# Two gate projections with stationary tokens, and every engine in written order

## The chip, the core and the metric

The kernel runs on one core of a Trainium2 chip. A core has a matrix engine (PE), a vector engine (DVE), an activation engine (ACT), a general engine (POOL) and a queue engine that issues the DMAs (SP). The metric is the device time of one execution in microseconds, as the median of several.

## The reference

One layer of a hybrid decoder, 256 tokens of width 1024, all in float32:

```python
xn = rmsnorm(h, norm_mix_g[l])
q_a, k_a, v_a, q_b, f_b, i_b, og_b, g_a, g_b = split_cols(xn @ w_in[l])
y_a = moba_attention(q_a, k_a, v_a, positions) @ w_br_attn[l]
y_b = hgrn2(q_b, f_b, i_b, og_b, lb_all[l], hgrn_norm_g[l]) @ w_br_hgrn[l]
merged = jax.nn.sigmoid(g_a) * y_a + jax.nn.sigmoid(g_b) * y_b
h = h + merged @ w_out[l]
h = h + memory_cross_attention(rmsnorm(h, norm_x_g[l]), ...)
h = h + (jax.nn.silu(gu[..., :FFN_HIDDEN]) * gu[..., FFN_HIDDEN:]) @ w_ffn_out[l]
return rmsnorm(h, final_norm_g)
```

Two of the nine projections matter here. The forget gate of the gated recurrence is `lb + (1 - lb) * sigmoid(f_b)`, and its query is `silu(q_b) * 128 ** -0.5`; each has 8 heads of 128 features. The output of the recurrence is normed per head, so a constant factor on the query only changes the epsilon of that norm. The attention branch has 16 heads of 64 with rotary embedding; with 256 tokens there is one causal block.

## The kernel before

All weights pass through the core once, cut into 97 slabs of 128 x 2048 floats (1 MB each) in the order of `plan()`. `prep` loads a slab into `raw` (two buffers) and splits it into two float32r parts: `hi` by ACT (line 177) and `lo = raw - hi` (line 180), of which DVE takes 1152 columns and POOL 896 (`POOL_COLS`). `hi` and `lo` have three buffers each. `nxt()` hands out the next slab and first runs `prep` up to `LEAD` = 2 slabs ahead, so the split of slab i+2 is written just before the matmuls of slab i. Each product is three matmuls, hi·hi, hi·lo and lo·hi.

There are two forms of a product. `gemm_f` ("F") keeps weights stationary and streams 256 tokens; its result has features on partitions. `gemm_t` ("T") keeps tokens stationary and streams 512 weight columns; its result has tokens on partitions, and two slabs (`kh` 0 and 1) make one result of 512 columns. The forget gate and the recurrence queries, the first eight slabs, are in F form, because the recurrence wants features on partitions (`fT`, `KS`, `QQ`, `QP`). The token scale of the first norm, `r_x`, is computed from the feature-major x by squares, additions and a matmul with ones, turned into a row (`rows_x`), and multiplied into each gate result.

Side work is written as generators. `tick()` runs after every slab: first what lies in `later`, then one step of each generator in `bg`. Such generators are `rope_tables` (sine and cosine), `hgrn` (18 steps of the recurrence's score matrix: `level_one`, `pair_levels`, `widen`, `level`), `attention` (calls `duo`, the softmax of two heads, at two of three ticks; a duo's probabilities are transposed one tick later, tile `aT`, and multiplied with the values two ticks later, tile `ao`), `hgrn_out` (per head group: recurrence output `ho`, copy, square, norm, then transposes `hT`), and `memory`.

PE's instructions are issued in the order written. For the other engines a scheduler in the compiler chooses the order:

```python
with tc.manual_schedule(engines={mybir.EngineType.PE}):
    build(tc, aps, out)
```

In `duo` the two heads stand one after the other, and in `hgrn_out` the power comes ahead of the product that it does not need:

```python
G.tensor_tensor(r, v, nhalf, op=ALU.pow)
...
G.tensor_tensor(sg, on, sg, op=ALU.mult)
V.tensor_tensor(sg, sg, r.unsqueeze(2).to_broadcast([128, 4, 128]), op=ALU.mult)
```

Of the kernel before, what the change touches and what calls it, by code (L numbers as in the profile page):

```python
# [10 lines left out]
F32 = mybir.dt.float32  # L11
# [16 lines left out]
POOL_COLS = 896  # L28
WARM = 18
# [82 lines left out]
def build(tc, A, out):  # L112
    nc = tc.nc
    V, SC, G, PE, SY = nc.vector, nc.scalar, nc.gpsimd, nc.tensor, nc.sync
    with ExitStack() as ctx:
# [42 lines left out]
        def prep(tags=None, pieces=2, raw=None):  # L158
            i = made[0]
            made[0] += 1  # L160
            if raw is None:
                raw = wr.tile([128, 2048], F32, name="raw", tag="raw")
            if tags is None:
                hi = wh.tile([128, 2048], F32R, name="hi", tag="hi")
                lo = wl.tile([128, 2048], F32R, name="lo", tag="lo")
            else:
                hi = big(tags[0], "hix", (128, 2048), F32R)
                lo = big(tags[1], "lox", (128, 2048), F32R)
            n = 2048 // pieces
            if pieces == 2:  # L170
                SY.dma_start(raw, A["w"][i])
            for c in range(pieces):
                a = slice(c * n, (c + 1) * n)
                if pieces > 2:
                    SY.dma_start(raw[:, a], A["w"][i][:, a])
                    yield
                SC.activation(hi[:, a], raw[:, a], AF.Copy)  # L177
                cut = (c + 1) * n - POOL_COLS // pieces
                for eng, b in ((V, slice(c * n, cut)), (G, slice(cut, (c + 1) * n))):
                    eng.tensor_tensor(lo[:, b], raw[:, b], hi[:, b].bitcast(F32), op=ALU.subtract)  # L180
# [128 lines left out]
        opening = [prep(pieces=4), prep(pieces=4, raw=big("B14", "raw1", (128, 2048)))]  # L309
        for c in range(4):  # L310
            SY.dma_start(xraw[:, 2 * c:2 * c + 2], A["xT"][:, 2 * c:2 * c + 2])
            for g in opening:
                next(g)
            for k in (2 * c, 2 * c + 1):
                g1 = gv[:, V_MIX + k:V_MIX + k + 1]
                if k % 2 == 0:
                    SC.activation(Xh[:, k], xraw[:, k], AF.Copy, scale=g1)
                else:
                    V.tensor_scalar(Xh[:, k], xraw[:, k], g1, None, op0=ALU.mult)
                V.scalar_tensor_tensor(Xl[:, k], xraw[:, k], g1, Xh[:, k].bitcast(F32),  # L320
                                       op0=ALU.mult, op1=ALU.subtract)
# [21 lines left out]

        def ev_f(c):
            def ev(ps):
                for m in range(2):
                    h = 2 * c + m
                    t = t2("fraw", (128, 256))
                    V.tensor_tensor(t, ps[m] if isinstance(ps, list) else ps[:, m], rows_x, op=ALU.mult)
                    SC.activation(t, t, AF.Sigmoid)  # L350
                    V.tensor_scalar(fT[:, 2 * h:2 * h + 2].rearrange("p a b -> p (a b)"), t,
                                    oml[:, h:h + 1], lbt[:, h:h + 1], op0=ALU.mult, op1=ALU.add)
                SC.activation(KS[:, 4 * c:4 * c + 4], fT[:, 4 * c:4 * c + 4], AF.Copy, scale=-1.0, bias=1.0)
            return ev

        def ev_q(c):
            def ev(ps):
                t = t2("qraw", (128, 2, 256))
                th = t2b("qth", (128, 2, 256))
                V.tensor_tensor(t, ps, bc(rows_x, 2, 1), op=ALU.mult)  # L360
                SC.activation(th, t, AF.Tanh, scale=0.5)
                a = slice(4 * c, 4 * c + 4)
                v4 = "p m (a b) -> p (m a) b"
                V.scalar_tensor_tensor(QQ[:, a, 64:192], th.rearrange(v4, a=2), 1.0,
                                       t.rearrange(v4, a=2), op0=ALU.add, op1=ALU.mult)
                G.tensor_tensor(QP[:, a], QQ[:, a, 64:192], fT[:, a], op=ALU.mult)
                odd = QP[:, a].rearrange("p a (b c) -> p a b c", c=2)[:, :, :, 1]
                SC.activation(QQ[:, a, 0:64], odd, AF.Copy)
            return ev

        ws = [by_k(ready.pop(i), 8) for i in range(2)]
        at[0] = 2
        pss = [[p.tile([128, 256], F32, name="psg", tag=n) for _ in range(2)]
               for p, n in ((mm, "mm"), (sm, "sm"))]
        SY.dma_start(cst, A["cst"])
        run(prep())
        SY.dma_start(lm, A["lm"])
        SY.dma_start(posi, A["pos"])
        for k in range(8):
            for i in range(2):  # L380
                for m in range(2):
                    f_part(pss[i][m], ws[i], X, m, (k,))
        for c in range(4):
            square(xraw, c)
        feature_sum(xraw)
        w2 = by_k(nxt(1), 8)
        ps2 = mm.tile([128, 2, 256], F32, name="psf", tag="mm")
        f_part(ps2[:, 0], w2, X, 0, range(8))
        r_x = feature_rstd(xraw, "x")
        f_part(ps2[:, 1], w2, X, 1, range(8))  # L390
        w3 = by_k(nxt(1), 8)
        ps3 = mm.tile([128, 2, 256], F32, name="psf", tag="mm")
        f_part(ps3[:, 0], w3, X, 0, range(8))
        f_part(ps3[:, 1], w3, X, 1, range(7))
        rows_x = rows_of(r_x, "x", "rowsA")
        f_part(ps3[:, 1], w3, X, 1, range(7, 8))
        for c, ps in enumerate(pss + [ps2, ps3]):
            ev_f(c)(ps)
        r_half = cp.tile([128, 2], F32, name="r_half")
        V.tensor_scalar(r_half, r_x, 0.5, None, op0=ALU.mult)  # L400

# [4 lines left out]
        def rope_tables():  # L406
            posf = small("posf", [2])
            V.tensor_copy(posf, posi)
            q = cp.tile([128, 6, 2, 32], F32, name="rt")
            ang, m, mh, ml, r, t = (q[:, i] for i in range(6))  # L410
            for i in range(2):
                V.tensor_scalar(ang[:, i], cst[:, C_IF:C_IF + 32], posf[:, i:i + 1], None, op0=ALU.mult)

            def rnd(o, src, c):
                V.tensor_scalar(o, src, c, None, op0=ALU.mult)
                V.tensor_scalar(o, o, RND, None, op0=ALU.add)
                V.tensor_scalar(o, o, RND, None, op0=ALU.subtract)
# [6 lines left out]
            V.tensor_scalar(mh, mh, 1024.0, None, op0=ALU.mult)  # L424
            V.tensor_tensor(ml, m, mh, op=ALU.subtract)
# [11 lines left out]
            V.tensor_scalar(t, r, lim, -TWO_PI, op0=ALU.is_gt, op1=ALU.mult)  # L437
            V.tensor_scalar(ml, r, -lim, TWO_PI, op0=ALU.is_lt, op1=ALU.mult)
            V.tensor_tensor(r, r, t, op=ALU.add)
            V.tensor_tensor(r, r, ml, op=ALU.add)  # L440
            yield 1
            V.tensor_scalar(r, r, lim, -lim, op0=ALU.min, op1=ALU.max)
            V.tensor_scalar(t, r, -1.0, None, op0=ALU.mult)
            V.tensor_tensor(t, t, r, op=ALU.max)
            V.tensor_scalar(t, t, -1.0, TWO_PI / 4, op0=ALU.mult, op1=ALU.add)
            SC.activation(m, r, AF.Sin)
            SC.activation(mh, t, AF.Sin)
            for i in range(2):
                rs = r_x[:, i:i + 1]
                for c in range(2):  # L450
                    V.tensor_scalar(Ct[:, i, c * 32:(c + 1) * 32], mh[:, i], rs, None, op0=ALU.mult)
                V.tensor_scalar(St[:, i, 0:32], m[:, i], rs, -1.0, op0=ALU.mult, op1=ALU.mult)
                V.tensor_scalar(St[:, i, 32:64], m[:, i], rs, None, op0=ALU.mult)
# [129 lines left out]
        def hgrn_out(obh, obl):  # L583
            for g in range(2):
                for t in range(2):
# [15 lines left out]
                    V.tensor_scalar(v, ssq, 1.0 / 128.0, 512.0 * EPS, op0=ALU.mult, op1=ALU.add)  # L601
# [16 lines left out]

        hg = hgrn()
        for c in range(4):  # L620
# [122 lines left out]
        drain(hg)  # L743
# [35 lines left out]
        SY.dma_start(H, A["xtok"])  # L779
# [329 lines left out]
```

## Time and profile before

| | |
|---|---|
| median of 3 runs | 639.62 us (639.62 to 640.02) |
| the profiled execution | 641.26 us, span 639.5 us |
| busy share of the span | PE 98%, DVE 63%, ACT 50%, POOL 58% |
| first matmul of the first slab | 7.39 us |
| end of the eight slabs of gate and queries | 65.8 us |
| last matmul | 632.1 us |

The span runs from the first to the last instruction of the profiled execution; its own time is 1.8 us longer. PE's busy time contains pipelined matmuls that overlap, so the price of a matmul is read from the distance between two starts.

### The profile page before, as it was taken

The numbers are of one execution on the slowest core, as the hardware profiler recorded it, in microseconds if no ns is written. First come the engines' busy times: TensorE is split into PE (matmuls) and PEld (weight loads), VectorE is DVE, ScalarE is ACT, GpSimd is POOL, SyncE is SP. The second block draws the span as 40 slices with busy tenths as digits, with TensorE's granted clock in tenths as the row PEclk, the third lists the DMA queues.
The fourth block names the chain that finished last, engine by engine and source line by source line (L and its number), as shares of the span: only waits on it lengthen the run. The fifth ranks groups of instructions, "written<-read, shape, count | busy, mean of one in ns | idle before, by whom it ended". The sixth has DMA issues, their size and how long they took to land.

```text
span 639.5 us, 9044 instructions
## 1 busy us (share of the span) xinstructions
PE 624.7 (98%) x3428; PEld 533.6 (83%) x3428; DVE 405.9 (63%) x713; ACT 321.5 (50%) x506; POOL 369.4 (58%) x258
## 2 busy tenths in 40 slices
PE   8989999999999999999999999999999999999995
PEld 7979888888887877778889999888888888888884
DVE  6996898789857777695556546764344444444433
ACT  5383564433368666673446445564444444444433
POOL 3468654376554664346766767656565555665552
PEclk9998999999999999999999999999999999999998
DMA  8634554444443333545545455462355554555511
GB/s 282 216 128 162 197 198 169 157 166 138 152 179 132 132 132 132 181 149 197 180 155 192 148 197 183 165 248 81 133 197 198 181 175 178 194 194 197 198 67 66
DMA packets 17036, 107.56 MB, mean 168 GB/s; under 512 B 2144, under 2 KB 2272, under 8 KB 4576
## 3 DMA queue, kind: packets, MB, share of 16 engines
q1 hardware_dynamic: 16992, 106.98, 47.2%
q8 instruction: 27, 0.44, 0.3%
q14 instruction: 17, 0.14, 0.1%
HBM read 105.92 MB, written 1.05 MB: 167 GB/s over the span
## 4 chain that ended last, share of the span: by engine, by line
PE 91%; DVE 3%; POOL 2%; issue 2%; DMA 1%; ACT 1%; SPq 0%; POOLq 0%; DVEq 0%
PE pst L220 13%; PE pst L222 13%; PE pst L221 13%; PE psi L222 6%; PE psi L220 6%; PE psi L221 6%; PE psf L217 3%; PE psf L216 3%; PE psf L215 3%; PE acc L222 3%; PE acc L220 3%; PE acc L221 3%; PE lp L524 2%; PE pso L220 1%; PE pso L222 1%
## 5 line engine op out<-in xcount | busy, mean ns | idle before, releaser
L180 POOL TENSOR_TENSOR lo<-raw,hi 128x448 fp32r<-128x448 f32 (+1 forms) x194 | 298.5, 1554 | 207.9 <-ACT hi L177 198.2
L177 ACT ACTIVATE hi<-raw 128x1024 fp32r<-128x1024 f32 (+1 forms) x194 | 195.6, 1036 | 189.6 <-PE pst L222 79.3
L180 DVE TENSOR_TENSOR lo<-raw,hi 128x576 fp32r<-128x576 f32 (+1 forms) x194 | 197.4, 1021 | 122.5 <-ACT hi L177 121.3
L220 PE MATMUL pst<-hi,Xh 128*128 128x512 f32 x224 | 90.5, 404 | 0.0
L222 PE MATMUL pst<-hi,Xl 128*128 128x512 f32 x224 | 87.4, 390 | 0.0
L221 PE MATMUL pst<-lo,Xh 128*128 128x512 f32 x224 | 87.3, 390 | 0.0
L220 PE MATMUL psi<-hi,h2h 128*128 128x512 f32 x176 | 69.6, 395 | 0.0
L222 PE MATMUL psi<-hi,h2l 128*128 128x512 f32 x176 | 68.6, 390 | 0.0
L221 PE MATMUL psi<-lo,h2h 128*128 128x512 f32 x176 | 68.5, 389 | 0.0
L222 PEld LDWEIGHTS pst<-hi,Xl 128*128 128x128 f32 x224 | 42.0, 188 | 9.0
L220 PEld LDWEIGHTS pst<-hi,Xh 128*128 128x128 f32 x224 | 42.1, 188 | 8.7 <-issue 0.7
L221 PEld LDWEIGHTS pst<-lo,Xh 128*128 128x128 f32 x224 | 42.1, 188 | 7.9
L222 PEld LDWEIGHTS psi<-hi,h2l 128*128 128x128 f32 x176 | 33.0, 188 | 7.1
L221 PEld LDWEIGHTS psi<-lo,h2h 128*128 128x128 f32 x176 | 33.1, 188 | 6.6
L220 PEld LDWEIGHTS psi<-hi,h2h 128*128 128x128 f32 x176 | 33.1, 188 | 6.5
L220 PE MATMUL acc<-hi,hid 128*128 128x512 f32 x88 | 34.3, 390 | 0.0
L222 PE MATMUL acc<-hi,hid 128*128 128x512 f32 x88 | 34.2, 389 | 0.0
L221 PE MATMUL acc<-lo,hid 128*128 128x512 f32 x88 | 34.2, 389 | 0.0
L217 PE MATMUL psf<-Xh,lo 128*128 128x256 f32 x96 | 29.3, 306 | 4.1 <-DVE lo L180 2.2
L215 PE MATMUL psf<-Xh,hi 128*128 128x256 f32 x96 | 28.6, 298 | 0.0
L216 PE MATMUL psf<-Xl,hi 128*128 128x256 f32 x96 | 28.3, 295 | 0.0
L1000 DVE SCALAR_TENSOR_TENSOR fu<-psi,r_h,fg 128x256 f32<-128x256 f32 x22 | 10.6, 484 | 26.0 <-ACT fg L998 25.8
(316 smaller groups left out, 1266.8 us busy)
## 6 DMA issues: line engine op xcount, KB each, us to landing
raw<-w SPq DMA_DIRECT2D x95, 1024.0 KB, 4.8
raw<-w SPq DMA_DIRECT2D x8, 256.0 KB, 5.6
xraw<-xT SPq DMA_DIRECT2D x4, 256.0 KB, 5.5
H<-xtok SPq DMA_DIRECT2D x1, 1024.0 KB, 8.7
mraw<-mT SPq DMA_DIRECT2D x1, 1024.0 KB, 5.6
out<-H SPq DMA_DIRECT2D x4, 256.0 KB, 2.2
gfin<-gfin SPq DMA_DIRECT2D x1, 512.0 KB, 6.5
cst<-cst SPq DMA_DIRECT2D x1, 272.0 KB, 5.7
```

The costliest lines, as they stand in the source:

```text
L177: SC.activation(hi[:, a], raw[:, a], AF.Copy)
L180: eng.tensor_tensor(lo[:, b], raw[:, b], hi[:, b].bitcast(F32), op=ALU.subtract)
L215: PE.matmul(ps, lh, rh, start=first, stop=False)
L216: PE.matmul(ps, lh, rl, start=False, stop=False)
L217: PE.matmul(ps, ll, rh, start=False, stop=last)
L220: PE.matmul(ps, xh, h, start=first, stop=False)
L221: PE.matmul(ps, xh, l, start=False, stop=False)
L222: PE.matmul(ps, xl, h, start=False, stop=last)
L524: PE.matmul(ps[:, j], KS[:, a0 + j], QQ[:, a0 + j], start=True, stop=True)
L1000: V.scalar_tensor_tensor(u, ps[:, 256:512], r, g, op0=ALU.mult, op1=ALU.mult)
```

## The change

Slabs 0 to 7 (forget gate, recurrence queries) go to T form. `turned` turns the token-major result back with PE transposes (four groups of eight), one or two ticks later, and evicts it from there. The gate's sigmoid becomes a tanh with the token scale inside the activation, `0.5 * (1 - lb)` and the offset in the eviction; the query's silu is a `Silu` activation (so the factor 2 that the old form carried is gone, and the epsilon of the head norm goes from 512 to 128 times). The squares of x come from the token-major input H, by ACT with an accumulator, and H is loaded at the start and not at the gates. The rotary tables are computed on POOL, with a product and a sum in place of each fused operation, and are spread over six ticks. For slabs 2 to 7 DVE takes all of `lo` (`ALONE`). The loads of x come in pieces of 1, 1, 2, 2 and 2 feature blocks. The recurrence's score steps start one slab later, and the draining call before its output is gone. ACT, DVE, POOL and SP, too, issue in the order written.

```diff
+ALONE = range(2, 8)
-    for name, base in (("f", 4), ("q", 3)):
-        order += [("F", "w_in", base * 1024 + c * 256) for c in range(4)]
-    for base in (5, 2, 0, 1, 6):
+    for base in (4, 3, 5, 2, 0, 1, 6):
...
-                cut = (c + 1) * n - POOL_COLS // pieces
+                cut = (c + 1) * n - (0 if i in ALONE else POOL_COLS // pieces)
...
+        PIECES = (0, 1, 2, 4, 6, 8)
+        for a, b in zip(PIECES, PIECES[1:]):
+            SY.dma_start(xraw[:, a:b], A["xT"][:, a:b])
+            for k in range(a, b):
+                next(opening[k // 4])
+                part_x(k)
...
+        def turned(th, c, use):
+            def turn():
+                for b in range(2):
+                    bk = bank("fT_", (128, 2, 256))
+                    for j in range(2):
+                        for t in range(2):
+                            PE.transpose(bk[:, j, t * 128:(t + 1) * 128],
+                                         th[t][:, (2 * b + j) * 128:(2 * b + j + 1) * 128], ident)
+                    use(4 * c + 2 * b, bk)
+            later.append(lambda: later.append(turn))
...
+            def ev(t, ps):
+                th[t] = t2("fth")
+                SC.activation(th[t], ps, AF.Tanh, scale=r_half[:, t:t + 1])
+                if t == 1:
+                    turned(th, c, use)
...
+                SC.activation(th[t], ps, AF.Silu, scale=r_x[:, t:t + 1])
...
-        for c in range(4):
-            square(xraw, c)
-        feature_sum(xraw)
...
+        f2 = [mm.tile([128, 512], F32, name="pst", tag="mm") for _ in range(2)]
+        w = by_k(nxt(), 4)
+        for t in range(2):
+            t_part(f2[t], w, X, t, 0)
+        ssqx = small("ssqx", [2])
+        junk = big("B9", "junk", (128, 2, 1024))
+        for t in range(2):
+            SC.activation(junk[:, t], H[:, t], AF.Square, accum_out=ssqx[:, t:t + 1])
+        r_x = rstd_of(ssqx, "x")
...
             def acc(o, a, c, b):
-                V.scalar_tensor_tensor(o, a, float(c), b, op0=ALU.mult, op1=ALU.add)
+                G.tensor_scalar(u, a, float(c), None, op0=ALU.mult)
+                G.tensor_tensor(o, u, b, op=ALU.add)
...
+        start(rt)
+        for c in range(2):
+            gemm_t(X, ev_q(c))
         hg = hgrn()
-        for c in range(4):
-            if c == 2:
-                start(hg)
-            gemm_f(X, ev_q(c), bank("psf", (128, 2, 256)) if c == 0 else None)
-        start(rt)
+        next(hg)
+        start(hg)
...
-        drain(hg)
...
-        SY.dma_start(H, A["xtok"])
...
-        with tc.manual_schedule(engines={mybir.EngineType.PE}):
+        with tc.manual_schedule(engines={mybir.EngineType.PE, mybir.EngineType.Activation, mybir.EngineType.DVE,
+                                         mybir.EngineType.Pool, mybir.EngineType.SP}):
             build(tc, aps, out)
```

More of the change, by code (lines that the diff above doesn't have):

```diff
@@ L156, in build, with prep @@
         made, at = [0], [0]
-        def prep(tags=None, pieces=2, raw=None):
+        def prep(tags=None, raw=None):
             i = made[0]
             made[0] += 1
+            first = i < 2
             if raw is None:
@@ L168, in prep @@
                 lo = big(tags[1], "lox", (128, 2048), F32R)
+            pieces = 4 if first else 2
             n = 2048 // pieces
-            if pieces == 2:
+            if not first:
                 SY.dma_start(raw, A["w"][i])
@@ L173, in prep @@
                 a = slice(c * n, (c + 1) * n)
-                if pieces > 2:
+                if first:
                     SY.dma_start(raw[:, a], A["w"][i][:, a])
@@ L308, in build, with part_x @@
             PE.matmul(warm, still[:, :128], still, start=True, stop=True)
-        opening = [prep(pieces=4), prep(pieces=4, raw=big("B14", "raw1", (128, 2048)))]
-        for c in range(4):
[L311 to L321, printed above, removed]
+        opening = [prep(), prep(raw=big("B14", "raw1", (128, 2048)))]
+        def part_x(k):
+            g1 = gv[:, V_MIX + k:V_MIX + k + 1]
+            if k % 2 == 0:
+                SC.activation(Xh[:, k], xraw[:, k], AF.Copy, scale=g1)
+            else:
+                V.tensor_scalar(Xh[:, k], xraw[:, k], g1, None, op0=ALU.mult)
+            V.scalar_tensor_tensor(Xl[:, k], xraw[:, k], g1, Xh[:, k].bitcast(F32),
+                                   op0=ALU.mult, op1=ALU.subtract)
+        PIECES = (0, 1, 2, 4, 6, 8)
[4 more added lines that the diff above has]
+                part_x(k)
         for g in opening:
@@ L342, in build @@
         QP = big("B3", "QP", (128, 16, 128))
-        def ev_f(c):
[L345 to L353, printed above, removed]
+        gate_a = cp.tile([128, 8], F32, name="gate_a")
@@ L393, in build @@
[L393 to L398, printed above, removed]
+            h, l = (z[:, k % 4] for z in ws[k // 4])
+            for t in range(2):
+                PE.matmul(pss[t], Xh[:, k, t * 128:(t + 1) * 128], h, start=k == 0, stop=False)
+                PE.matmul(pss[t], Xl[:, k, t * 128:(t + 1) * 128], h, start=False, stop=False)
@@ new lines, in build @@
+            for t in range(2):
+                PE.matmul(pss[t], Xh[:, k, t * 128:(t + 1) * 128], l, start=False, stop=k == 7)
+        f2 = [mm.tile([128, 512], F32, name="pst", tag="mm") for _ in range(2)]
+        w = by_k(nxt(), 4)
+        for t in range(2):
+            t_part(f2[t], w, X, t, 0)
+        ssqx = small("ssqx", [2])
+        junk = big("B9", "junk", (128, 2, 1024))
+        for t in range(2):
+            SC.activation(junk[:, t], H[:, t], AF.Square, accum_out=ssqx[:, t:t + 1])
@@ L399, in build @@
+        r_x = rstd_of(ssqx, "x")
         r_half = cp.tile([128, 2], F32, name="r_half")
         V.tensor_scalar(r_half, r_x, 0.5, None, op0=ALU.mult)
+        for t in range(2):
+            ev_f0 = ev_f(0) if t == 0 else ev_f0
+            ev_f0(t, pss[t])
+        tick()
+        w = by_k(nxt(), 4)
+        ev_f1 = ev_f(1)
+        for t in range(2):
+            t_part(f2[t], w, X, t, 1)
+            ev_f1(t, f2[t])
+        tick()
         Ct = cp.tile([128, 2, 64], F32, name="Ct")
```

100 lines of the change are left out of this document (54 added, 46 removed).

## The prediction

> **What bounds the kernel now.** I read the page's busy times first, then who waited for whom on PE, then the stretches of time, and last the timelines of PE, DVE, ACT and POOL.
>
> ```profile
> PE 624.7 (98%) x3428; PEld 533.6 (83%) x3428; DVE 405.9 (63%) x713; ACT 321.5 (50%) x506; POOL 369.4 (58%) x258
> ```
> ```profile
> PE psf L217 <- DVE lo L180: 2.2, 3, 0.9
> PE psf L217 <- POOL lo L180: 1.8, 1, 1.8
> ```
> ```profile
> 21.78:65.82 44.04, 39.93 (x297) 38.40 (x296) 36.23 (x81) 22.38 (x34) 28.17 (x28) 0.92 0.45 164
> 44.31:47.72 3.41, 1.44 (x10) 1.03 (x8) 3.41 (x7) 2.84 (x4) 3.27 (x4) 0.97 0.00 0
> 47.50:50.90 3.40, 2.76 (x13) 2.76 (x14) 2.30 (x3) 0.00 (x0) 3.40 (x4) 0.50 0.56 149
> 50.90:54.30 3.40, 3.40 (x18) 3.40 (x18) 0.00 (x0) 0.00 (x0) 3.16 (x6) 0.50 0.38 159
> ```
> PE is the bound: 98% busy, and the two waits shown are all of its waits after the first block. They lie in the stage that the change rewrites: the forget gate's last two blocks and the four query blocks, 21.78 to 65.82 us. (A block is one 1 MB slab of weights.) Columns of a stretch are its length, then busy us of PE, weight load, DVE, ACT, POOL, then the granted clock. In 44.31 to 47.72 DVE is busy without a break while PE works 1.44 of 3.41 us; then the clock stands at 0.50 for 6.8 us. So what this stage pays is DVE arriving late, and then a slow clock. Behind it PE is full until its last matmul: there the change can only lose, unless it takes matmuls away, and it takes none away.
>
> **Part 1: matmuls.** The first eight blocks go from 48 matmuls of 256 columns to 24 of 512. Start times on PE give the price of each; the last row is eight transposes of 128 columns.
>
> ```profile
> 16.02 0.28 PE L215 MATMUL psg<-Xh,hi 128*128 128x256 f32 x1
> 16.14 0.28 PE L216 MATMUL psg<-Xl,hi 128*128 128x256 f32 x1
> ...
> 71.24 0.39 PE L220 MATMUL pst<-hi,Xh 128*128 128x512 f32 x1
> 71.47 0.39 PE L221 MATMUL pst<-lo,Xh 128*128 128x512 f32 x1
> ```
> ```profile
> 140.30 0.87 PE rT L656 x8
> ```
> 0.12 us x 48 = 5.76 us per block against 0.227 x 24 = 5.44: 0.3 us gained per block. The new tokens-by-features result has to be turned: four groups of eight transposes, 0.87 us each, say 1.0 with the change of operand type, so 4.0 us are added. By PE work alone, then, this is worth about nothing (eight blocks give 2.5); what counts is the stall and the clock.
>
> **Part 2: the front as a sum.** I leave the first two blocks where they end now, at 21.78 (the smaller pieces of x bring the first matmul a few tenths forward; the last quarter of slab 0 is now split after slab 1's third, which can take them back). Six blocks follow, 6 x 5.44 = 32.6, and four turns, 4.0: 36.6 us for what takes 44.04. Does everything else arrive? These rows carry it:
>
> ```profile
> raw<-w SPq DMA_DIRECT2D x95, 1024.0 KB, 4.8
> ```
> ```profile
> L177 ACT ACTIVATE hi<-raw 128x1024 fp32r<-128x1024 f32 x186 | 191.0, 1054 | 188.2 <-PE pst L222 79.3 <-PE psi L222 35.5 <-PE acc L222 28.0
> L753 ACT ACTIVATE tbt<-pst,r_half 128x512 f32<-128x512 f32 x4 | 2.7, 684 | 3.2 <-PE pst L222 3.0
> ```
> ```profile
> L271 POOL TENSOR_TENSOR r_x<-v__359,nhalf 128x2 f32<-128x2 f32 x1 | 0.7, 707 | 4.2 <-DVE v__359 L269 4.2
> ```
> Written order puts the squares of x, hence r_x, hence the forget gate's tanh, behind ACT's split of slab 4. That slab's buffer frees when slab 2 is split, about 20.5; 4.8 us to land gives 25.3; two halves of 1.05 give 27.4; two squares of 1024 columns, 1.05 plus about 0.2 for the accumulator each, 29.9; mean, power (0.7) and halving, 31.2; two tanh of 0.68, 32.6. PE wants to turn that gate at 21.8 + 2 x 5.44 = 32.7. The two meet; I allow 0.4 us of wait, so the front is 37.0 instead of 44.0: **-7.0 us**. If the slab lands 2 us later, -5; if the first blocks also gain a microsecond or two, -9.
>
> Removed from DVE: the rotary chain's small operations, the additions of the squares, the row scaling of eight gates and four queries. Added: all of `lo` for slabs 2 to 7. Alone, and beside POOL, a 576-column `lo` takes:
>
> ```profile
> 28.65 0.74 DVE L180 TENSOR_TENSOR lo<-raw,hi 128x576 fp32r<-128x576 f32 x1
> ...
> 35.87 1.44 DVE L180 TENSOR_TENSOR lo<-raw,hi 128x576 fp32r<-128x576 f32 x1 [0.19 <-ACT hi L177]
> ```
> ```profile
> L496 POOL TENSOR_TENSOR Tt<-Tt 128x64 f32<-128x64 f32 x2 | 0.6, 294 | 0.2
> ```
> Scaled to 1024 columns that is 1.3 to 2.6 us, 2.6 to 5.1 per slab, in a block of 5.44 plus a turn of 1.0 every other block or oftener, with slabs split two blocks ahead: it is hidden at the lower price, and nearly so at the upper. The rotary chain on POOL is about 55 operations near 0.3 us, 16 us spread over six blocks; nobody needs the tables before slab 16. [...] Early loading of H costs one 1 MB transfer, moved from one place to another.
>
> **Part 3: all engines as written.** This is where I expect the gain to go back. Today the scheduler weaves `lo` and other work into the waits of a softmax or a head norm. In written order each wait stands on DVE. The group that matters is `duo` (two heads' softmax, one after the other) followed in the same tick by a step of `hgrn_out`, then by the next `lo`. A duo, by its pieces:
>
> ```profile
> 212.81 0.28 DVE L679 CUSTOM_DVE_ANT_0 ap<-as,cst 128x128 f32<-128x128 f32 x1
> ...
> 213.01 0.42 DVE L679 CUSTOM_DVE_ANT_0 ap<-as,cst 128x256 f32<-128x256 f32 x1
> ...
> 216.47 0.16 DVE L682 TENSOR_SCALAR anm<-amx 128x2 f32<-128x2 f32 x1
> ...
> 217.68 0.17 DVE L686 RECIPROCAL asum<-asum 128x2 f32<-128x2 f32 x1 [0.40 <-ACT ap L684]
> 217.88 0.55 DVE L688 TENSOR_SCALAR ap<-ap,asum 128x128 f32<-128x128 f32 x2
> ```
> ```profile
> 222.54 0.40 ACT L684 ACTIVATE ap<-ap,anm 128x128 f32<-128x128 f32 x1 [0.34 <-DVE anm L682]
> ...
> 223.34 0.19 ACT L684 ACTIVATION_READ_ACCUMULATOR ap<-ap,anm 128x1 f32 x1
> ```
> Per head: reductions to 213.43 and the negation 0.15 make 0.77; exponentials from 222.54 to 223.53, 0.99, with DVE standing; reciprocal and scaling 0.75; 0.1 for the handshakes: 2.6 us, 5.2 for the two. A head-norm step:
>
> ```profile
> 225.28 0.58 ACT L596 ACTIVATE hon<-ho 128x512 f32<-128x512 f32 x1
> 225.88 0.63 ACT L598 ACTIVATE hsq<-hon 128x512 f32<-128x512 f32 x1
> ```
> ```profile
> 218.35 0.68 DVE L600 TENSOR_REDUCE hss<-hsq 128x4 f32<-128x512 f32 x1
> ...
> 220.38 0.69 DVE L606 TENSOR_TENSOR sog<-sog,hr 128x512 f32<-128x512 f32 x1 [1.15 <-POOL hr L602]
> ```
> ```profile
> 225.93 1.29 POOL L605 TENSOR_TENSOR sog<-hon,sog 128x512 f32<-128x512 f32 x1 [2.33 <-ACT hon L596]
> 228.25 1.01 POOL L602 TENSOR_TENSOR hr<-hv,nhalf 128x4 f32<-128x4 f32 x1 [1.02 <-DVE hv L601]
> ```
> Now L605 runs before L602 and DVE waits 1.15 us. In written order L605 stands behind the power, so DVE waits 2.5: 218.35 to 220.38, plus 1.3, plus 0.69 is 4.1, plus 0.5 for copy and square behind the last exponential, 4.6. With the slab's two `lo` (2 x 1.03 on the mean) a tick with both costs DVE 12 us. PE's ticks with such work last
>
> ```profile
> 210.56:218.67 8.11, 8.11 (x50) 6.46 (x50) 6.39 (x20) 5.87 (x14) 4.09 (x3) 1.00 0.52 156
> 218.67:227.74 9.07, 9.07 (x56) 7.32 (x54) 7.82 (x22) 6.51 (x16) 4.59 (x4) 1.00 0.40 145
> 227.74:235.72 7.98, 7.98 (x47) 6.41 (x46) 5.67 (x9) 4.86 (x8) 6.48 (x5) 1.00 0.32 111
> 235.72:244.73 9.01, 9.01 (x58) 7.36 (x58) 7.25 (x22) 5.83 (x14) 3.91 (x4) 1.00 0.36 119
> ```
> Ticks 1, 2 and 4 of these hold a duo and a norm step, 3 a norm step alone, 5 a duo. PE transposes a duo's probabilities one tick after its scores. Counting from 210.56: the first duo runs 2.2 to 7.4, norm to 12.1, `lo` to 14.2, the second duo to 19.4; PE wants it at 8.1 + 9.1 + 0.8 (another duo's output) = 18.0: **1.4 us**. Then norm 24.0, `lo` 26.1, norm 30.6, `lo` 32.7, third duo (0.4 of a split before it) 38.3; PE, now 1.4 late, wants it at 35.6: **2.7 us**. Norm 43.1, `lo` 45.2, fourth duo 50.4; PE wants it at 46.6: **3.8 us**. Together +7.9. With chains 15% shorter it is about 3, 15% longer 13. The next duos start on time again.
>
> Stalls of this size can drop the clock: the 6.8 us at half clock, shown above, behind a stretch with 1.44 of 3.41 us busy, lost 3.4. Half of that, 1.7, goes into the sum. [...]
>
> Elsewhere (gated recurrence, cross attention, feed-forward, end) each chain fits its tick in written order by my count; ends 0 and +3, value 0.
>
> **Sum.** -7.0 + 7.9 + 1.7 = +2.6 us. The profiled execution took 641.26 with a span of 639.5; the median is 639.62, and the difference carries over: 639.6 + 2.6 = **642.2 us**.
>
> **The rivals.** *A, the attention hides its waits:* the duo with norm and `lo` stays under PE's 8.5 us per tick instead of 12. For it speaks that before, with `lo` woven in, a duo was already done only a few tenths before its transposes; against it that weaving is what the change forbids. It decides at about 9 us. Then only the front counts: 632.6. *B, the front pays little:* POOL's small operations hold `lo` at its upper price, DVE needs 5.1 plus the evictions, a block runs up to 1 us late, four of them lose 4 us: front -3, total 646.2. *C, the stalls come without a half clock:* PE keeps working on either side of each, and the row that tripped was PE at 42% for a whole 3.4 us; -7.0 + 7.9 = +0.9, 640.5. [...] *D, written order is close to what the scheduler does anyway:* as A, and counted with it.
>
> **Chances.** Forecast 0.45 (its own range 638 to 647), A with D 0.27, B 0.15, C 0.13. About 0.2%, 1.3 us, is what a measurement of this kernel tells from no change. Faster: A, with 0.08 of the edges of forecast and C, 0.35. Same: 0.13, mostly C. Slower: 0.52. The range 632.0 to 648.5 reaches to A's middle and past B's.
>
> **What the changed profile would show.** Right: `pst` matmuls of X at 0.227 us from the start; the first `level_one` matmul (L478's line) not later than 65.8 - 7 plus its one-block shift; no half clock in the front; PE waiting on `aT` for the scaling of `ap` by DVE, three waits of 1 to 5 us some 200 us in; DVE waiting on POOL's `sog` 2.5 us. Wrong: no `aT` waits (A), or PE waits on `lo` or `fth` before 60 us (B). A wait of several microseconds elsewhere would break the zero that I gave to the rest.

## The result

| | median, us | lowest to highest | ratio to before (95% interval) |
|---|---|---|---|
| before | 639.62 | 639.25 to 640.02 | |
| after | 667.15 | 666.5 to 667.9 | 1.0431 [1.0413, 1.0449] |

The change makes the kernel 4.3% slower. Its profiled execution has a span of 665.1 us against 639.5, so 25.6 us have to be found in the two profiles (the medians differ by 27.5, mostly because the profiled execution before, 641.26 us, was 1.6 above its median). Two lines of the page and the list of what PE waited for, after:

```profile
span 665.1 us, 8697 instructions
PE 631.9 (95%) x3262; PEld 527.2 (79%) x3262; DVE 409.5 (62%) x653; ACT 325.0 (49%) x509; POOL 371.5 (56%) x294
```
```profile
PE psg L420 <- ACT hi L178: 4.7, 2, 3.6
PE aT L742 <- DVE ap L734: 3.6, 3, 1.9
PE ssq L298 <- issue: 3.0, 1, 3.0
PE psi L222 <- ACT hi L178: 2.5, 1, 2.5
PE hT L659 <- DVE amx L725: 2.4, 1, 2.4
PE psi L222 <- ACT h2h L1020: 1.9, 1, 1.9
...
PE ho L639 <- ACT pT L744: 1.3, 1, 1.3
PE psg L423 <- DVE lo L182: 1.1, 1, 1.1
PE hT L659 <- DVE obl L267: 1.1, 1, 1.1
```

Before, PE had two kinds of wait after its first block, 4.0 us together, both in the front. Now there are over a dozen, none longer than 3.6 us and spread from 10 to 480 us, nearly all on ACT or DVE (a transfer stands behind some of them, as will be seen). PE falls from 98% busy to 95%, and its busy time still grows by 7.2 us, though the program has 166 fewer matmuls (one of 512 columns does the work of two of 256): part of them ran at half clock. The windows view over six stretches of after (columns as in the prediction: length, busy us of PE, weight load, DVE, ACT, POOL, granted clock, DMA share, GB/s):

```profile
14.90:21.90 7.00, 5.79 (x13) 4.14 (x14) 6.47 (x17) 2.81 (x5) 2.04 (x3) 0.52 0.57 226
185.60:280.05 94.45, 84.80 (x459) 65.38 (x459) 61.20 (x164) 56.25 (x125) 39.73 (x28) 0.96 0.32 117
247.22:254.05 6.83, 6.23 (x22) 4.71 (x22) 4.38 (x5) 2.61 (x4) 4.90 (x4) 0.50 0.00 0
308.66:312.07 3.41, 3.41 (x10) 2.64 (x9) 2.80 (x6) 1.37 (x2) 0.81 (x2) 0.50 0.67 221
465.68:469.09 3.41, 3.41 (x9) 2.59 (x9) 3.41 (x3) 1.80 (x2) 3.41 (x3) 0.50 0.04 5
479.33:482.74 3.41, 3.41 (x9) 2.64 (x8) 1.44 (x3) 1.92 (x3) 3.05 (x3) 0.50 0.62 262
```

Where before had one stretch at 0.50, after has five, each behind a wait of PE, 24 us long in all; they cost half their length, 12 us, against 3.4 before.

That comparison leaves out one thing. The clock records of before begin only at 13.37 us; ahead of that the view prints 1.00, but the matmuls themselves start 0.21 us apart and not 0.12. From PE's timeline of before:

```profile
8.48 0.41 PE L216 MATMUL psg<-Xl,hi 128*128 128x256 f32 x1
8.70 0.41 PE L217 MATMUL psg<-Xh,lo 128*128 128x256 f32 x1
```

So before ran the first 26 matmuls of its opening at half speed too, which is about 26 x 0.09 = 2.4 us. After has its matmuls at full speed from the first one at 6.55 us, up to 15.1 us (those of 512 columns at 10.12, 10.34 and 10.57 us start 0.23 apart).

I divide the run where the same matmul first starts in each kernel: the third block's first matmul, the first attention score (`as`), the first matmul on `obh` (the recurrence's output), on `mh` (the two branches merged), into `pso` (the last projection added to H), into `psi` (feed-forward, in) and into `acc` (feed-forward, out). Stage lengths in us, from PE's start times:

| stage | before | after | difference |
|---|---|---|---|
| opening, two blocks | 21.78 | 25.91 | +4.1 |
| to the first attention score | 167.52 | 159.69 | -7.8 |
| attention and head norm | 80.34 | 94.45 | +14.1 |
| products on `obh` and `oah`, memory norm | 47.98 | 52.76 | +4.8 |
| memory and cross attention | 105.85 | 105.90 | 0 |
| `pso`, addition to H | 23.23 | 25.98 | +2.75 |
| first feed-forward block | 22.72 | 29.69 | +7.0 |
| the rest | 170.08 | 170.72 | +0.6 |

The rewritten front brings what it was meant to. It is lost again at five places, four of them in text that the change does not touch: only the order of issue differs there.

**The opening.** Timelines of ACT and of PE, after:

```profile
13.18 0.51 ACT L316 ACTIVATE Xh<-xraw,gv 128x256 fp32r<-128x256 f32 x1
13.83 1.77 ACT L178 ACTIVATE hi<-raw 128x512 fp32r<-128x512 f32 x3
```
```profile
15.03 0.74 PE L420 MATMUL psg<-hi,Xh 128*128 128x512 f32 x1 [3.60 <-ACT hi L178]
...
26.14 0.39 PE L223 MATMUL pst<-lo,Xh 128*128 128x512 f32 x1
26.37 0.39 PE L224 MATMUL pst<-hi,Xl 128*128 128x512 f32 x1
```

Slab 0's last quarter is the last of the three splits in the row at 13.83, because `run(opening[0])` stands behind all pieces of slab 1. PE stands 3.60 us for it and then runs at 0.52.

The late opening hides a second delay. DVE, ACT and PE, after:

```profile
20.13 2.35 DVE L182 TENSOR_TENSOR lo<-raw,hi 128x1024 fp32r<-128x1024 f32 x2
```
```profile
29.05 2.01 ACT L178 ACTIVATE hi<-raw 128x1024 fp32r<-128x1024 f32 x2 [4.07 <-DMA raw<-w]
34.41 1.27 ACT L385 ACTIVATE fth<-psg,r_half 128x512 f32<-128x512 f32 x2 [1.28 <-DVE r_half L434]
```
```profile
36.80 0.60 PE L363 MATMUL fT__359<-cst,fth 128*128 128x128 f32 x4
```

DVE's `lo` of slab 2 releases that slab's buffer at 22.5 us, and only then can slab 4's load start: it is issued at 22.51 and lands at 28.94. ACT stands for it until 29.05, and the gate's tanh, with the squares of x behind that split, ends at 35.7. PE comes to turn the gate at 36.80, so here it does not wait.

**The attention.** DVE and POOL in the first tick with a softmax pair and a norm step:

```profile
214.06 0.69 DVE L646 TENSOR_REDUCE hss<-hsq 128x4 f32<-128x512 f32 x1 [0.40 <-ACT hsq L644]
...
217.35 1.60 DVE L652 TENSOR_TENSOR sog<-sog,hr 128x512 f32<-128x512 f32 x1 [2.40 <-POOL sog L651]
```
```profile
216.05 1.26 POOL L651 TENSOR_TENSOR sog<-hon,sog 128x512 f32<-128x512 f32 x1
217.27 2.68 POOL L182 TENSOR_TENSOR lo<-raw,hi 128x448 fp32r<-128x448 f32 x2
```

DVE stands 2.40 us for POOL, and then its multiplication takes 1.60 us instead of 0.69: POOL's `lo` starts 0.08 us ahead of it and runs right across it. All four norm steps show this (1.60 to 1.64 us); before, one of four did (1.62 us, with POOL's `lo` starting 0.06 us ahead) and the other three took 0.69. In the same stretch PE's idle time is 94.45 - 84.80 = 9.65 us.

**Memory norm.** DVE's sum of squares stands behind a `lo`, and PE's `ssq` matmul, in written order too, blocks PE:

```profile
303.40 1.44 DVE L182 TENSOR_TENSOR lo<-raw,hi 128x576 fp32r<-128x576 f32 x1 [0.19 <-ACT hi L178]
304.76 1.62 DVE L292 TENSOR_TENSOR mraw<-mraw 128x512 f32<-128x512 f32 x1
306.41 1.23 DVE L293 TENSOR_TENSOR mraw<-mraw 128x256 f32<-128x256 f32 x1
```
```profile
307.75 0.58 PE L298 MATMUL ssq<-ones,mraw 128*128 128x1 f32 x4 [2.95 <-issue]
```

The view names no releaser ("issue"); the end of DVE's sum at 307.64 is the one that fits.

**First feed-forward block.** ACT, after:

```profile
462.96 0.63 ACT L876 ACTIVATE hjunk<-H 128x512 f32<-128x512 f32 x1 [2.21 <-DVE H L872]
...
463.59 3.88 ACT L178 ACTIVATE hi<-raw 128x1024 fp32r<-128x1024 f32 x4
472.86 2.01 ACT L178 ACTIVATE hi<-raw 128x1024 fp32r<-128x1024 f32 x2 [5.38 <-DMA raw<-w]
476.97 0.63 ACT L1020 ACTIVATE h2h<-h2g 128x512 fp32r<-128x512 f32 x1 [2.10 <-DVE h2g L1019]
```

No slab is split between the squares of H: the four halves follow in one go at 463.59, when PE already wants them (it waits 2.5 us there). The next slab's load could start only behind them (issued at 468.07 us, landed at 472.75), so ACT stands 5.38 us for it. `h2h` needs no load, but it needs `h2g` of DVE, and `h2g` stands in DVE's queue behind that slab's `lo`:

```profile
474.90 1.43 DVE L182 TENSOR_TENSOR lo<-raw,hi 128x576 fp32r<-128x576 f32 x1 [0.19 <-ACT hi L178]
476.26 0.68 DVE L1019 TENSOR_TENSOR h2g<-h2T,gv 128x512 f32<-128x512 f32 x1
```

PE waits 1.9 us for `h2h`.

### The profile page after: what moved, and what is told of

Same layout as the page of the kernel before. It is cut to its first block, busy times and chain, and to the rows that moved or that the text cites. A ratio compares the mean times of both kernels' runs of the same rounds, so it can differ in the third digit from the quotient of the medians.

```text
span 665.1 us, 8697 instructions
## 1 busy us (share of the span) xinstructions
PE 631.9 (95%) x3262; PEld 527.2 (79%) x3262; DVE 409.5 (62%) x653; ACT 325.0 (49%) x509; POOL 371.5 (56%) x294
## 4 chain that ended last, share of the span: by engine, by line
PE 83%; issue 4%; DVE 4%; POOL 3%; ACT 3%; DMA 2%; SPq 1%; POOLq 0%; ACTq 0%; DVEq 0%
PE pst L222 12%; PE pst L224 12%; PE pst L223 12%; PE psi L224 6%; PE psi L222 6%; PE psi L223 6%; PE acc L222 3%; PE acc L224 3%; PE acc L223 3%; PE psf L218 2%; PE psf L217 2%; PE psf L219 2%; DMA raw<-w 2%; POOL lo L182 2%; PE lp L570 2%
## 5 line engine op out<-in xcount | busy, mean ns | idle before, releaser
L182 POOL TENSOR_TENSOR lo<-raw,hi 128x448 fp32r<-128x448 f32 (+1 forms) x182 | 285.8, 1591 | 188.3 <-ACT hi L178 184.7
L182 DVE TENSOR_TENSOR lo<-raw,hi 128x576 fp32r<-128x576 f32 (+2 forms) x194 | 215.7, 1124 | 101.6 <-ACT hi L178 100.9
L222 PE MATMUL pst<-hi,Xh 128*128 128x512 f32 x272 | 110.0, 405 | 0.0
L223 PE MATMUL pst<-lo,Xh 128*128 128x512 f32 x272 | 106.7, 392 | 0.0
L224 PE MATMUL pst<-hi,Xl 128*128 128x512 f32 x272 | 106.6, 392 | 0.0
L224 PEld LDWEIGHTS pst<-hi,Xl 128*128 128x128 f32 x272 | 51.5, 189 | 11.0
L222 PEld LDWEIGHTS pst<-hi,Xh 128*128 128x128 f32 x272 | 51.6, 190 | 10.7 <-issue 0.7
L223 PEld LDWEIGHTS pst<-lo,Xh 128*128 128x128 f32 x272 | 51.6, 190 | 9.8
L730 ACT ACTIVATE ap<-ap,anm 128x128 f32<-128x128 f32 (+1 forms) x32 | 14.3, 448 | 36.4 <-DVE anm L728 36.4
L1042 ACT ACTIVATE fg<-psi,r_h 128x256 f32<-128x256 f32 x22 | 10.4, 475 | 27.2 <-PE psi L224 27.2
```

The lines of the kernel that those rows point to most:

```text
L222: PE.matmul(ps, xh, h, start=first, stop=False)
L223: PE.matmul(ps, xh, l, start=False, stop=False)
L224: PE.matmul(ps, xl, h, start=False, stop=last)
L730: SC.activation(p[:, u:w], p[:, u:w], AF.Exp, scale=0.125, bias=nm[:, i:i + 1], accum_out=sums[:, i:i + 1])
L1042: SC.activation(g, ps[:, 0:256], AF.Silu, scale=r)
```

## The experiments

The theory: written order on ACT, DVE, POOL and SP costs the time at these five places, waits and half clocks together, and the new arithmetic is a gain. The first rival: the new arithmetic (gates with stationary tokens, turns, rotary work on POOL) is itself dear. The second: SP's order of the loads is the cause. Each median stands beside runs of the kernel before on the same chip, 639.4 to 639.7 us.

**PE alone in written order** (`e1_pe_only`), the rest of the change kept:

```diff
-        with tc.manual_schedule(engines={mybir.EngineType.PE, mybir.EngineType.Activation, mybir.EngineType.DVE,
-                                         mybir.EngineType.Pool, mybir.EngineType.SP}):
+        with tc.manual_schedule(engines={mybir.EngineType.PE}):
```

> The changed kernel, but only PE keeps its written order; ACT, DVE, POOL and SP are ordered by the scheduler as before. Theory (written order on the other engines makes five stalls, in the opening, attention, memory norm, wo block and first feed-forward block, and the half clock behind them): the stalls from 185 us on mostly go, the front's gain of about 8 us stays, 630 to 637. Rival 1 (the new arithmetic itself costs: token-stationary gates, the turns, rotary work on POOL beside DVE): the stalls stay, over 655. Rival 2 (SP's written order of the loads is the cause): PE's waits go where a DMA had ended them, and the attention's 14 us stay.

Measured: 643.68 us, 1.0062 [1.0047, 1.0077]. All the waits behind the front go: attention 79.96, memory 47.96, `pso` 23.28, feed-forward 22.75 us. But the front, opening to the first score, takes 191.39 us where after takes 185.60: 6 us worse, not equal. ACT and PE there:

```profile
36.60 1.17 ACT L381 ACTIVATE KS<-fT 128x512 f32<-128x512 f32 x2
47.69 0.26 ACT L489 ACTIVATE rt<-rt 128x64 f32<-128x64 f32 x1 [9.92 <-POOL rt L487]
...
51.22 1.99 ACT L178 ACTIVATE hi<-raw 128x1024 fp32r<-128x1024 f32 x2
```
```profile
52.31 0.80 PE L222 MATMUL pst<-hi,Xh 128*128 128x512 f32 x1 [6.75 <-ACT hi L178]
```

The scheduler put a rotary step of ACT ahead of a slab's split, and that step waited 9.92 us for the chain of small operations on POOL.

**The same with the rotary tables on DVE** (`e13_rope_dve`): in the kernel above, the tables' operations are issued on `V` again.

```diff
 def rope_tables():
-                G.tensor_scalar(ang[:, i], cst[:, C_IF:C_IF + 32], posf[:, i:i + 1], None, op0=ALU.mult)
+                V.tensor_scalar(ang[:, i], cst[:, C_IF:C_IF + 32], posf[:, i:i + 1], None, op0=ALU.mult)
...
```

> The changed kernel with only PE in written order (643.7 so far), and one edit: the small operations of the rotary tables go to DVE, where the kernel before had them, and not to POOL. Theory (with the scheduler's order, ACT's rotary step waited 9.9 us for POOL with a slab's split behind it, and PE 6.8 us and a half clock): that stall goes, the level-one matmul starts at 64 to 66 instead of 73.4, total 633 to 637. Rival (the scheduler places the splits late whichever engine does the tables): another stall in the front, 641 or more.

Measured: 632.53 us, 0.9891 [0.9876, 0.9906], the fastest of all. From its page and from PE's waits:

```profile
span 630.0 us, 8681 instructions
PE 620.0 (98%) x3262; PEld 521.7 (83%) x3262; DVE 398.1 (63%) x705; ACT 324.5 (52%) x509; POOL 346.4 (55%) x242
```
```profile
PE warm L310 <- DVE still L307: 1.6, 1, 1.6
PE psg L421 <- DVE Xl L319: 0.6, 1, 0.6
PE psg L420 <- ACT hi L178: 0.5, 1, 0.5
```

After the opening PE waits for nothing, and no stretch from 10.95 us, where its clock records begin, to the last microseconds shows a half clock. The level-one matmul starts at 61.97 us, earlier than expected, and everything behind the front has the length that it had before. So the first rival is out: token-stationary gates, turns and token-major squares, with the other edits of the text, are worth 7 us net.

**The kernel before in written order** (`e2_before_all`): the opposite edit to the first, on the old text.

> The kernel before, with ACT, DVE, POOL and SP in written order too, and nothing else of the change. Theory: the same stalls as in the changed kernel from the attention to the first feed-forward block, 14 + 5 + 10 us, and some more in the front, where the old text was woven by the scheduler: 668 to 685. Rival 1 (the new arithmetic costs): near 640 to 645. Rival 2 (loads' order): a loss of under 15 us, with DMA ends before the waits.

Measured: 687.12 us, 1.0746 [1.0728, 1.0764]. Attention 95.04, memory 51.58, `pso` 25.90, feed-forward 29.86 us: within 1.2 us the lengths of after, without any of the new arithmetic. To the first attention score it takes 202.73 us against 189.30, one wait of 7.37 us for a split in it. Written order costs the old text 47.5 us by the medians; the profiled execution, 683.43 us, was the fastest of five, so its stages show only 42 of them.

**The two chains of the attention.** In `e6_duo` the softmax pair goes stage by stage; in `e7_norm` POOL's order is turned round and DVE's last multiplication comes a tick later; `e8_att` has both.

```diff
# e6_duo: reductions of both heads; then exponentials of both; then scalings of both
                 V.tensor_scalar(nm, mx, -0.125, None, op0=ALU.mult)
+            for p, nm, sums in mid:
                 for i, (u, w) in enumerate(parts):
...
# e7_norm
-                    G.tensor_tensor(r, v, nhalf, op=ALU.pow)
...
                     G.tensor_tensor(sg, on, sg, op=ALU.mult)
-                    V.tensor_tensor(sg, sg, r.unsqueeze(2).to_broadcast([128, 4, 128]), op=ALU.mult)
+                    G.tensor_tensor(r, v, nhalf, op=ALU.pow)
+                    last = (sg, r)
                     yield 1
+                    sg, r = last
+                    V.tensor_tensor(sg, sg, r.unsqueeze(2).to_broadcast([128, 4, 128]), op=ALU.mult)
```

> The changed kernel with two edits of written order: the two heads of a softmax pair go stage by stage instead of one after the other, and the head norm's gate product stands ahead of the power on POOL, with the last multiplication on DVE a tick later. Theory (DVE stands still in these chains): the attention's stretch, 94.5 us, comes back to 80 to 84, with no half clock in it: 667.2 - 11 to 14 = 653 to 656. Rivals (POOL beside DVE makes each operation slower, or a transfer comes late): the stretch stays above 90 us, total over 662.

> The changed kernel with one edit: the two heads of a softmax pair go stage by stage (both reductions, both exponentials, both scalings). Both edits of the attention together gave -11.3. Theory (two chains of equal weight; DVE stood 2 x 1 us for the exponentials in each pair): 667.2 - 4 to 6 = 661 to 663. Rival 1 (the norm step is the whole cause): 666 to 667. Rival 2 (the pair is the whole cause): 655 to 657.

> The changed kernel with one edit: the head norm's gate product stands ahead of the power on POOL, and DVE's last multiplication comes a tick later, so that DVE no longer stands 2.4 us per step. Theory (two chains of equal weight): 661 to 663. Rival 1 (the norm step is the whole cause): 655 to 657. Rival 2 (the pair is the whole cause): 666 to 667.

| | median, us | ratio to before | attention stretch, us |
|---|---|---|---|
| after | 667.15 | 1.0431 [1.0413, 1.0449] | 94.45 |
| softmax pair | 659.35 | 1.0309 [1.0286, 1.0331] | 85.31 |
| head norm | 658.40 | 1.0301 [1.0283, 1.0318] | 84.94 |
| both | 655.85 | 1.0255 [1.0240, 1.0270] | 80.29 |

Both together take the stretch back to the scheduler's 80. Either alone already brings 9 of the 14 us, more than expected: the two share DVE's one queue, and it is their sum that runs past PE's tick. PE's idle time in the stretch goes from 9.65 us to 4.1 (pair) or 4.3 (norm) and to 0.4 with both, so each takes away over half; and either alone also takes away the half clock in the stretch, 3.4 us, which is most of why the two single gains add up to more than both together. Neither is "the" cause. The DMA rival is out for this stretch: no load was touched.

**Three single edits of order.**

```diff
# e3_opening: slab 0's last quarter ahead of slab 1's pieces
                 next(opening[k // 4])
+                if k == 4:
+                    run(opening[0])
                 part_x(k)
...
# e4_ffn_prep: two slabs split inside the wo block
+                if (t, c) in ((0, 1), (1, 0)):
+                    run(prep())
                 add_h(t, c, ps, None, ssq2)
# e5_memory: the ssq matmul one tick later
             feature_sum(raw)
             yield 1
+            yield 1
```

> The changed kernel with one edit: slab 0's last quarter is split ahead of slab 1's pieces. Theory (ACT's written order makes PE wait 4.7 us there, and a half clock follows): the first two blocks end near 20 instead of 25.9, but the gate's tanh, behind slab 4's load, then makes PE wait some 2.5 us; net -2 to -4 at the first level-one matmul, total 663 to 666. Rival (the loads set the opening): the blocks end at 25 or later, total 667.

Measured: 666.39 us, 1.0414 [1.0399, 1.0430]; its interval overlaps that of after. The two blocks end at 19.69 us instead of 25.91, as expected, and then PE waits 2.7 us for the gate's tanh, runs at half clock behind that (0.60 on the mean from 34.85 to 39.10 us), and starts the level-one matmul at 67.69 us (after: 67.55). All 6.2 us are given back at the next steps. The chain is in ACT's and PE's timelines:

```profile
28.69 2.01 ACT L178 ACTIVATE hi<-raw 128x1024 fp32r<-128x1024 f32 x2 [4.86 <-DMA raw<-w]
30.60 1.04 ACT L432 ACTIVATE junk<-H 128x1024 f32<-128x1024 f32 x1
```
```profile
34.79 0.33 PE L364 MATMUL fT__359<-cst,fth 128*128 128x128 f32 x1 [2.70 <-ACT fth L386]
```

> The changed kernel with one edit: two slabs are split inside the wo block, ahead of the additions to H, instead of behind them. Theory (the splits of the first feed-forward slabs stand behind ACT's last square and then wait for their load): the waits from the wo block to the first accumulation, 2.8 + 7.0 us with two half clocks, go: 667.2 - 9.7 = 656 to 659. Rival (the additions to H and the turns set it, the splits only stand beside): 663 or more.

Measured: 658.67 us, 1.0296 [1.0279, 1.0314]: -8.5. `pso` to `acc` takes 46.8 us instead of 55.7. Where the splits stand was the cause; the loads behind them move with them, so this edit does not tell the splits from their loads. No run freezes or frees SP's order alone.

> The changed kernel with one edit: the memory's sum of squares on PE comes one tick later. Theory (PE waited 2.95 us for DVE's sum, queued behind a split, and lost 1.7 us more at half clock): 667.2 - 4.8 = 661.5 to 663.5. Rival (DVE is late throughout that stretch, and the wait moves to the next step): 666 or more.

Measured: 666.42 us, 1.0422 [1.0403, 1.0441], not told apart from after. The wait at `ssq` is gone from PE's list, it does not move to a later step, and its stage is 50.45 us instead of 52.76; but a half clock came up at its start that after does not have. This profiled execution, 668.51 us, was the slowest of four, and its opening, in unchanged text, ended at 27.57 us, 1.7 later than in after: of the 0.7 us between the medians the profile can't say more. PE's timeline and the windows, first of this kernel, then of after:

```profile
281.24 1.11 PE L659 MATMUL hT<-cst,sog 128*128 128x128 f32 x4 [2.39 <-DVE amx L725]
```
```profile
280.40:287.20 6.80, 5.96 (x16) 4.86 (x17) 3.90 (x19) 3.67 (x13) 1.23 (x1) 0.50 0.80 320
```
```profile
279.64 0.66 PE L659 MATMUL hT<-cst,sog 128*128 128x128 f32 x4 [2.40 <-DVE amx L725]
```
```profile
279.60:286.40 6.80, 6.76 (x36) 5.30 (x36) 3.46 (x14) 3.77 (x12) 0.42 (x1) 1.00 0.70 267
```

The wait is the same, 2.39 and 2.40 us, in unchanged text; the clock behind it is 0.50 in one run and 1.00 in the other. My theory had the wait right and took its half clock for a fixed part of its price, which it is not (the last section has more on this).

**All orders mended** (`e9_fixed`): the five edits above together.

> The changed kernel with all written orders mended: the two edits of the attention; slab 0's last quarter split ahead of slab 1's pieces (opening, -4); the memory's sum of squares one tick later (-5); the first feed-forward slabs split before the H squares of the wo block (-8 to -10). Theory: the sum is 667.2 - 14 - 4 - 5 - 9 = 635, range 631 to 641, with no half clock after the first 15 us or one at most. Rivals: a stall that moves on to the next place leaves 645 to 655; new arithmetic as the cause leaves 655 or more.

Measured: 639.77 us, 1.0002 [0.9992, 1.0012]; the profiled execution took 638.42 with a span of 636.6 and no half clock before its end. The five edits, measured in four runs (-0.8, -8.5, -0.7, and -11.3 for the attention's two), add up to -21.3; all together bring -27.4. The profiles show part of the difference: with the attention alone mended, the wait at `ssq` grew from 2.95 to 3.81 us and the memory stage from 52.76 to 54.73, and the opening, untouched in three of the four, ended between 25.2 and 27.6 us against 25.91. What is left in the front is the tanh, 2.5 us late.

**And the squares of x ahead of slab 4's split** (`e10_squares`):

```diff
-        w = by_k(nxt(), 4)
-        for t in range(2):
-            t_part(f2[t], w, X, t, 0)
         ssqx = small("ssqx", [2])
...
         V.tensor_scalar(r_half, r_x, 0.5, None, op0=ALU.mult)
+        w = by_k(nxt(), 4)
+        for t in range(2):
+            t_part(f2[t], w, X, t, 0)
```

> The kernel with all written orders mended, and the squares of x with their mean ahead of slab 4's split. Theory (the gate's tanh came 2.5 us late behind slab 4's load): the first level-one matmul at 63.5 to 64.5 instead of 66.0, total 639.8 - 2 = 637 to 638, between the kernel before and the one with written order in the front alone. Rival (slab 4's split is late in its turn): no change, 639.5 to 640.5.

Measured: 635.49 us, 0.9942 [0.9927, 0.9957]; level-one at 63.20 us instead of 66.03. Of the 4.3 us gained on the last kernel's median, 2.8 are seen between the two profiles; the rest is that the last kernel's profiled execution, 638.42 us, was the fastest of its ten. So all engines in written order is no loss as such: this text in that order beats the kernel before. It does not beat the scheduler, which with the tables on DVE (`e13_rope_dve`) is 3.0 us faster still.

**Written order in the front alone** (`e11_front`), with the edits of the opening and of the squares:

```diff
+        front = tc.manual_schedule(engines={mybir.EngineType.Activation, mybir.EngineType.DVE,
+                                            mybir.EngineType.Pool, mybir.EngineType.SP})
+        front.__enter__()
         Xh, Xl = big("B1", "Xh", dt=F32R), big("B2", "Xl", dt=F32R)
...
         drain(rt)
+        front.__exit__(None, None, None)
```

> Written order on all engines only up to the last value block, the scheduler's order on ACT, DVE, POOL and SP behind it; in the front, slab 0's last quarter is split ahead of slab 1's pieces, and the squares of x with their mean stand ahead of slab 4's split. Theory (written order is a gain in the front and a loss from the attention on): the first level-one matmul starts near 63.5 (65.8 in the kernel before), and what follows takes the 568.0 us that it took with PE alone in written order (641.4 - 73.4): a span of 631 to 633, total 632 to 635, faster than the kernel before. Rival 1 (the new arithmetic takes back the gain behind the front): 638 or more. Rival 2 (the front cannot go below its loads): the level-one matmul stays at 66 to 68, total 635 to 638.

Measured: 635.21 us, 0.9927 [0.9912, 0.9942], the span 633.9. Level-one starts at 64.42 us, with a stretch of half clock from 21.8 to 25.2 us ahead of it, which cost 1.7 us, and the memory and cross attention take 1.1 us longer than elsewhere (a wait of 0.9 at `xT`). The theory's sign and place hold; the span came 1 us above its range.

## Why the prediction was wrong

It said 642.2 and at most 648.5; slower was right, the size was not. Step by step:

- **The front: right in size, in part by luck.** -7.0 foreseen from 21.78 us on; -7.8 measured to the first score. The 0.227 us per matmul are there (the rows at 26.14 and 26.37), and four turns fit beside it. But the chain to the tanh was foreseen 3 us too short: slab 4's buffer free at 20.5 and the tanh done at 32.6, where the runs have 22.5 (DVE's `lo` releases it, not ACT's split) and 35.7. This cost nothing only because the opening was late and PE came at 36.80. With the opening as foreseen PE would have wanted the gate at 32.7 and waited about 2 us (an estimate from these rows), as it waits 2.70 in `e3_opening`; the prediction's own branch for a late slab, -5, was the nearer one. Rival B asked for late `lo` in the front, and PE waits for none there after the opening.
- **The opening: left at 21.78, and it took 4.1 us more.** The prediction saw the cause, slab 0's last quarter behind slab 1's third, and gave it a few tenths. The row at 15.03 has 3.60, another wait of 1.08 follows, and the half clock from 15.1 to 21.9 us costs 3.4. That this makes 4.1 and not 8 us is because the 21.78 held a half clock too, which the prediction had not seen (matmuls at 0.21 us up to 13.4), and because the first matmul now starts 0.84 us earlier. The foreseen level-one start, 58.8 plus a block of 5.44, was 64.2; it came at 67.55. The mended opening alone would not have paid: the tanh then ends last.
- **The attention: mechanism right, size short.** Foreseen 7.9 of waits and 1.7 of half clock; measured 9.65 idle and 4.5 more of busy PE, 3.4 of it half clock. The three waits foreseen at `aT` are there, but come to 3.6 us and not 7.9. DVE's wait for POOL was foreseen at 2.5 and is 2.40, a pair at 2.6 us per head as in the rows. Mis-sized was the norm step, 5.3 us on DVE (213.67 to 218.95) and not 4.6, with the slab's two `lo` at 2.4 and not 2.1 behind it: DVE's last multiplication at 0.69 is 1.60 beside POOL's `lo`, which written order puts right behind the gate product. The other 6 us of waits stand at whatever DVE or ACT owes next (`ho`, `hT`, `as`).
- **"Elsewhere each chain fits its tick, value 0": this step failed.** The three places behind the attention cost 4.8 + 2.75 + 7.0 = 14.5 us, the greater part of the miss of 25 (the opening has 4.1 of it and the attention 4.5; 2 more are the distance between medians and profiles). The zero rested on a count of busy time per tick and quoted no row; what counts is the position of an instruction in its queue: the splits behind the last square of H, the sum of squares and `h2g` behind a `lo`. The bound of +3 came from nothing, and so the range was too short.
- **The half clock.** Half of one was allowed; 12 us of loss stand in the trace, 8.5 more than in before's records and some 6 more when before's opening is counted, spread over the stages above. Behind the opening, waits under 3 us were enough (the longest, at `ssq`, took 2.95): wherever 2.0 us or more of waiting fell into one step of 3.41, half clock followed, as the last section counts.
- **Rivals A, C and D** fall: the attention does not hide its waits, the half clock comes, and written order is far from what the scheduler does (+47.5 us on the old text, +23.5 on the new: 643.7 to 667.2).

The change is thus three things: new arithmetic, with the smaller edits of the text, that is worth -7 us (632.5), rotary tables on POOL that cost +11.2 under the scheduler (643.7; what they cost in written order no run shows by itself), and an order that costs +23.5 in places that nobody had rewritten for it.

## What to carry to other kernels

When an engine's order is frozen, every place in the program where a scheduler used to lift an instruction over a waiting one is part of the change: go through each engine's queue, also in text that the diff does not show, and ask what stands behind each wait. Give no stage a zero because its busy time fits; quote the row of the instruction that comes last. And change arithmetic and order in separate steps: here one was a gain that the other hid.

## What the runs showed of the hardware

- The granted clock changed only on a grid: within each of the 14 traces all its changes lie whole multiples of 3.41 us apart (in after, from 15.12 us on: 2, 66, 2, 16, 1, 45, 1, 3 and 1 of them). Sort the waits in PE's timelines into the steps of that grid: a step at full clock with 2.0 us or more of waiting was followed by half clock in all 33 cases, one with less than 1.5 us in none, and between these in 7 of 17. So in these traces a wait's place counted as well as its length. The 2.70 us at the gate's turn in `e3_opening` lie in one step, and the clock fell; the 2.48 in `e9_fixed` lie across two, as 1.03 and 1.45, and it did not. At `hT` the 2.39 us of `e5_memory` put 1.59 into one step that had 0.31 already, and it fell; the 2.40 of after put 0.70 into one and 1.70 into the next, and it did not. What decides between 1.5 and 2.0 us stays open.
- A DVE multiplication with two operands of 512 columns went from 0.69 to 1.60 us when POOL's `lo` started just ahead of it (0.69 to 1.62 within the kernel before).
- The opening of unchanged text ended between 25.2 and 27.6 us in six profiled kernels, with 1.7 to 5.1 us lost at half clock in it: a single profile can't weigh an edit there.
